# Two equal token groups and one pool of large tiles in a decoder step on one Trainium2 core

## The chip, the cores and the metric

The kernel runs on 1 core of one Trainium2 chip, in one launch. The metric is the device time of that launch in microseconds; the median of three runs stands for a kernel. The engines are called as the profile calls them: PE (TensorE), DVE (VectorE), ACT (ScalarE), POOL (GpSimd), SP (SyncE, which here only issues the weight loads).

## What is computed

One inference step of a decoder of two layers, all in fp32, for a prompt of 512 tokens and a sample of 8 sequences with 8 new tokens each (64). The model is 1024 wide. For each layer, cut from the reference:

```python
rq, rk, rv, rg, sq, sk, sv, mq, g_r, g_s, g_m = in_proj(x, w_in[l], pos)     # rotary on rq, rk, sq, sk
ret_o = retention(rq, rk, rv)              # 8 heads; the sample starts from a state that is given
swa_o = sliding_window(sq, sk, sv, sinks)  # 8 heads, 2 of keys and values, window 128
mem_o = mem_attend(mq, mk, mv)             # 4 heads, 256 memory tokens
ret_b = (silu(rg) * group_norm(ret_o)) @ w_br_ret
swa_b, mem_b = swa_o @ w_br_swa, mem_o @ w_br_mem
merged = sigmoid(g_r) * ret_b + sigmoid(g_s) * swa_b + sigmoid(g_m) * mem_b
x = layer_norm(ALPHA * x + merged @ w_out)
x = layer_norm(ALPHA * x + square(relu(x @ w_up)) @ w_down)
```

The prompt's memory keys and values come from `mem_prompt @ w_mem_kv`; each sample sequence has its own 256, cached, which are loaded. Outputs are the 576 tokens, and the new states, keys and values of each layer.

## The kernel before, in words

Features lie on partitions, tokens along the columns. All 576 tokens go through each weight once. The weights are cut into 154 units a layer (`unit_order`), 128 x 8 x 128 numbers each (512 KB). A unit is loaded by SP (`fetch`, 509) and split into a rounded high part and the rest, the low part (`split`, 515): a cast and a subtraction, or for `w_up` and `w_down` two casts and an accumulating DMA on POOL's queue. `gemm` (569) multiplies a unit by one group of tokens: for each of its 8 slices high by high, low by high and high by low, 24 matmuls that sum up in one PSUM bank. Three banks of tag g take turns for this.

The tokens stand in two groups (`NG`, `OFF`): A has the first 256 tokens of the prompt, B the other 256 and all 64 of the sample (320). `both` (589) runs a unit for A and then for B. The prompt's columns are worked on by `retention` (872), `swa_prompt` (1071) and `mem_prompt` (1202), the sample's by parts of `retention`, by `swa_sample` (1141) and `mem_sample` (1276), whose loads of cached keys (in_mck) and values (in_mcv) are issued on POOL's queue by `mem_load` (1260).

Large tiles come from two pools: tag A has 25 slots of 4096 bytes a partition (raw units, high parts, most low parts, everything of group A), tag B 15 of 5120 (everything of group B, and a few low parts by a rule in `split`). A new tile gets a slot that is free by the program's order, and what first writes it waits for the last reader of the tile before.

The order on each engine is made while the program is built. `run` (553) emits the matmul steps; after every sixth matmul of a unit it lets a filler advance, which gives out the next pieces of the branches, the norm and the weight splits, by a small clock of estimated times. Where an operation may run on two engines (`soonest`, 485; `pick`, 491; `rounded`, 495), that clock chooses: a subtraction goes to DVE or POOL, a cast to ACT or DVE. `plan` (204) estimates when each unit is used. So other widths change the order of many small operations and the engine of some. Between the layers the last norm of layer 0 (`norm_ev`) and the first units of layer 1 lie beside each other.

```python
def pick(self, *ins, bias=0.0):
    n = ins[0].free_size()
    return self.soonest((("vector", 0.068 + n / 960.0 + bias), ("gpsimd", 0.15 + n / 480.0)), *ins)
```

Of the kernel before, what the change touches and what calls it, by code (L numbers as in the profile page):

```python
# [17 lines left out]
P = 128  # L18
# [8 lines left out]
NG = {"A": 256, "B": 320}  # L27
OFF = {"A": 0, "B": 256}
# [14 lines left out]
N_A = 25  # L43
N_B = 15
# [89 lines left out]
def make_consts():  # L134
# [4 lines left out]
    pos = np.concatenate([np.arange(SEQ), np.tile(PAST + np.arange(NT), NB)]).astype(np.float32)  # L139
# [58 lines left out]

def mm_us(n):
    return n / 2400.0 + 0.0025  # L200


def plan():
    a, b = 24 * mm_us(256), 24 * mm_us(320)
    t, out = 0.0, []
    order = unit_order()
    for l in range(DEPTH):
        i = 0
        while i < UNITS:
            k = order[i][0]  # L210
            if k in ("mk", "mv"):
                out.append(t)
                t += a
# [4 lines left out]
            elif k == "rv":  # L218
                out += [t, t]
                t += 4.67 * a  # L220
# [195 lines left out]
class Builder:  # L416
# [35 lines left out]
    def u(self, n=320):  # L452
        return self.tile([P, 320], tag="u", bufs=5)[:, :n]

    def tt(self):
        return self.tile([P, 320], tag="t", bufs=4)
# [52 lines left out]
    def fetch(self, u):  # L509
        self.raw[u] = self.tile([P, 8, P], tag="A")  # L510
# [82 lines left out]
    def pair_tiles(self, dt=F32):  # L593
        return {"A": self.tile([P, 4, 256], dt, tag="A"), "B": self.tile([P, 4, 320], dt, tag="B")}

    def feat_tiles(self, nt):
        r = {}
        for g in "AB":
            r[g] = {"h": [], "l": []}
            for k in "hl":  # L600
                for j in range(nt):
                    r[g][k].append(self.tile([P, 4, NG[g]], F32R, tag=g))
        return r

    def load_x(self, X):
# [5 lines left out]
        def part(g, j):  # L611
            raw = self.tile([P, 4, NG[g]], tag=g)
# [9 lines left out]
        def split():  # L622
            for i in range(4):
# [5 lines left out]
                h = self.tile([P, 4, NG[g]], F32R, tag=g)  # L629
                lo = self.tile([P, 4, NG[g]], F32R, tag=g)  # L630
# [70 lines left out]
    def norm_ev(self, g, y, l, gi, eps, out, scale=None, bias=1.0):  # L701
# [33 lines left out]
        def half():  # L735
            c = st.pop("c")
            V.tensor_tensor(y[0], y[0], c.unsqueeze(1).to_broadcast([P, 4, n]), ALU.subtract)
            sq = self.tile([P, 4, n], tag=g)
# [7 lines left out]
        def last():  # L746
# [4 lines left out]
            t = self.tile([P, 320], tag="ln", bufs=2)[:, :n]  # L751
# [8 lines left out]
            r0 = self.tile([P, 320], tag="ln", bufs=2)[:, :n]  # L760
# [7 lines left out]
            a = self.tile([P, 320], tag="ln", bufs=2)[:, :n]  # L768
# [27 lines left out]
            if out is not None:  # L796
                out[g]["h"] += [self.tile([P, 4, n], F32R, tag=g) for _ in range(2)]
                out[g]["l"] += [self.tile([P, 4, n], F32R, tag=g) for _ in range(2)]
# [64 lines left out]

    def rope_evac(self, ps, out, o, n):
# [7 lines left out]
    def retention(self, l, p, qk, rv, sg, GR):  # L872
# [11 lines left out]
        yield Pe((qk, rv))  # L884
        v2 = self.tile([P, 2, 256], F32R)
        self.split_into(v2[:64, 0], v2[:64, 1], rv[:64, 4, :])
# [9 lines left out]
        for e in range(2):  # L896
            r = slice(e * 64, e * 64 + 64)
            for c in range(4):
                cs = slice(c * P, (c + 1) * P)
                T.matmul(pq[e][:, cs], lhsT=k[r, cs], rhs=q[r, cs], start=True, stop=True)  # L900
# [8 lines left out]
        for c in range(4):  # L909
            cs = slice(c * P, (c + 1) * P)  # L910
            T.transpose(pk[:, cs], k[:, cs], ident)
        px = [self.bank("a"), self.bank("a")]
        for e in range(2):
            r = slice(e * 64, e * 64 + 64)
            T.matmul(px[e][:64, P:P + 64], lhsT=k[r, 512:576], rhs=q[r, 512:576], start=True, stop=True)
        T.transpose(px[0][:64, 0:P], k[:, 512:576], ident)
# [17 lines left out]
        V.tensor_tensor(kq[:, 1].rearrange("p (c i) -> p c i", c=4), q[:, 0:512].rearrange("p (c i) -> p c i", c=4),  # L934
# [8 lines left out]
        for f in range(2):  # L943
            for e in range(2):
                r = slice(e * 64, e * 64 + 64)
                dst = self.qz[f * 64:f * 64 + 64, e, f * 32:f * 32 + 288].rearrange("p (b c) -> p b c", b=4)[:, :, 0:8]
                V.tensor_tensor(dst, q[r, 512 + f * 32:544 + f * 32].rearrange("p (b t) -> p b t", b=4),
# [11 lines left out]
        for bb in range(5):  # L959
            for e in range(2):  # L960
# [4 lines left out]
                else:  # L965
                    T.matmul(o, lhsT=ks[:, 256 + e * 64:320 + e * 64], rhs=rv[:64, 4, e * P:(e + 1) * P],
# [34 lines left out]
        gs = self.tile([P, P], tag="u", bufs=5)  # L1001
# [11 lines left out]
        wt = self.tile([P, 2, 512])  # L1013
        ws = self.tile([P, 2, 64], tag="ws", bufs=1)
# [763 lines left out]
```

## Time and profile before

| | |
|---|---|
| median of three runs | 2186.92 us (2186.02 to 2187.66) |
| profiled execution | 2185.91 us |
| its span | 2184.1 us |
| PE busy | 2147.9 us (98%) |
| DVE, ACT, POOL busy | 1060.2, 846.9, 411.2 us |
| HBM, read and written | 99 GB/s over the span |

The page has the span, each engine's busy time, the wait that ended an engine's idle time, and for each instruction its start and length. Matmuls are pipelined: the length of one overlaps the next, so their pace is read from start to start. The helper that records operations gives all of them one line, L331, so the rows are told apart by tile names and shapes (numbers left out). DVE and POOL rows of 128x1024 that read and write A are mostly the low parts of weight units.

### The profile page before, as it was taken

The page shows a single profiled execution, that of the slowest core. Times are in us where ns is not written, and L with a number is a line of the kernel's source. Part 1 is how long each engine was busy: PE and PEld are TensorE (multiplying, and loading weights), DVE is VectorE, ACT ScalarE, POOL GpSimd, SP SyncE. Part 2 cuts the span into 40 slices and gives each one's busy share as a digit, 9 for nine tenths or more (in the row PEclk, how much of TensorE's full clock was granted, in tenths as well). Part 3 has the DMA queues.
Part 4 walks back from the last instruction along what each step waited for, and adds up shares of the span by engine and source line. Part 5 has one row for each costly group of instructions (what it writes and reads, how often), then busy time and mean ns, then how long its engine had stood idle before and what let it go on. Part 6 is the DMA issues. An engine that isn't in the chain of part 4 may idle for free. (4 is left out here: it accounts for less than half of the span.)

```text
span 2184.1 us, 39229 instructions
## 1 busy us (share of the span) xinstructions
PE 2147.9 (98%) x16466; PEld 2089.6 (96%) x16466; DVE 1060.2 (49%) x2164; ACT 846.9 (39%) x1581; POOL 411.2 (19%) x400
## 2 busy tenths in 40 slices
PE   9999999999999999999999999999999999999996
PEld 9999999999999999999989998999999999999996
DVE  6666765455566111111876668554555751111127
ACT  3222234232146454636342221442221573636362
POOL 0222300011033111111432223000210321111113
PEclk9999999999999999999999999999999999999999
DMA  8222212334255867676452222123443557676661
GB/s 308 78 90 86 91 49 69 116 135 137 98 169 126 201 143 185 153 195 161 125 178 84 84 84 83 59 68 107 145 153 124 144 126 195 148 187 159 174 150 45
DMA packets 85168, 284.56 MB, mean 130 GB/s; under 512 B 9280, under 2 KB 19008, under 8 KB 84928
## 3 DMA queue, kind: packets, MB, share of 16 engines
q1 hardware_dynamic: 50944, 168.27, 22.2%
q0 software_dynamic: 28960, 105.92, 22.0%
q10 hardware_dynamic: 5088, 7.87, 1.1%
q8 instruction: 129, 2.11, 0.4%
q14 instruction: 47, 0.39, 0.1%
HBM read 200.89 MB, written 15.99 MB: 99 GB/s over the span
## 5 line engine op out<-in xcount | busy, mean ns | idle before, releaser
L331 PE MATMUL pg<-B,A 128*128 128x320 f32 x5920 | 1024.7, 310 | 2.4 <-DVE A L331 1.4
L331 PE MATMUL pg<-A,A 128*128 128x256 f32 (+1 forms) x6720 | 961.1, 286 | 12.1 <-DVE A L331 5.5
L331 PEld LDWEIGHTS pg<-A,A 128*128 128x128 f32 x6720 | 891.2, 192 | 28.9 <-issue 12.8
L331 PEld LDWEIGHTS pg<-B,A 128*128 128x128 f32 x5920 | 903.9, 188 | 7.5 <-issue 3.4
L331 ACT CAST A<-A 128x1024 fp32r<-128x1024 f32 (+4 forms) x316 | 294.0, 943 | 208.1 <-DVE A L331 73.1
L331 PE MATMUL pg<-A,B 128*128 128x256 f32 x1088 | 248.0, 283 | 0.0
L331 PE MATMUL pg<-B,B 128*128 128x320 f32 x704 | 217.5, 309 | 0.0
L331 DVE TENSOR_TENSOR A<-A,A 128x1024 fp32r<-128x1024 f32 (+3 forms) x173 | 191.1, 1115 | 49.6 <-ACT A L331 46.2
L331 PEld LDWEIGHTS pg<-A,B 128*128 128x128 f32 x1088 | 181.8, 192 | 0.0
L331 ACT ACTIVATE t<-pg 128x256 f32<-128x256 f32 (+1 forms) x128 | 52.5, 410 | 290.7 <-PE pg L331 290.5
L331 POOL TENSOR_TENSOR A<-A,A 128x1024 fp32r<-128x1024 f32 (+2 forms) x40 | 84.5, 2117 | 331.7 <-ACT A L331 273.6
L331 PEld LDWEIGHTS pg<-B,B 128*128 128x128 f32 x704 | 132.4, 188 | 0.0
L331 DVE TENSOR_TENSOR B<-u,B 128x320 fp32r<-128x320 f32 x80 | 39.4, 492 | 190.0 <-ACT B L331 190.0
L331 POOL DMA_DIRECT2D A<-A x64 | 55.7, 870 | 354.5 <-ACT u L331 177.1
L331 ACT ACTIVATE u<-pg 128x320 f32<-128x320 f32 (+1 forms) x128 | 51.4, 401 | 162.3 <-PE pg L331 162.1
L331 POOL DMA_DIRECT2D B<-A x64 | 55.0, 860 | 260.2 <-ACT B L331 115.8
L331 DVE TENSOR_TENSOR A<-u,A 128x256 fp32r<-128x256 f32 x72 | 30.5, 423 | 136.8 <-ACT A L331 129.0
L331 ACT ACTIVATE A<-A 128x1024 fp32r<-128x1024 f32 (+1 forms) x70 | 73.9, 1055 | 52.6 <-DMA B<-A 34.9
L331 DVE TENSOR_TENSOR B<-B,pg 128x320 f32<-128x320 f32 x56 | 27.0, 485 | 117.2 <-PE pg L331 117.1
L331 DVE TENSOR_TENSOR B<-B,u 128x256 f32<-128x256 f32 (+3 forms) x84 | 75.6, 908 | 2.4
L331 POOL TENSOR_TENSOR A<-A,cst 128x512 fp32r<-128x512 f32 x32 | 43.7, 1391 | 152.4 <-ACT A L331 152.4
L331 ACT ACTIVATE B<-A 128x1024 fp32r<-128x1024 f32 x64 | 67.4, 1053 | 0.0
(203 smaller groups left out, 1722.4 us busy)
## 6 DMA issues: line engine op xcount, KB each, us to landing
A<-in_wall SPq DMA_DIRECT2D x305, 512.0 KB, 3.5
B<-A POOLq DMA_DIRECT2D x64, 512.0 KB, 5.2
A<-A POOLq DMA_DIRECT2D x64, 512.0 KB, 5.3
A<-in_mck POOLq DMA_DIRECT2D x16, 512.0 KB, 4.2
A<-in_mcv POOLq DMA_DIRECT2D x16, 512.0 KB, 6.3
A<-in_s POOLq DMA_DIRECT2D x8, 512.0 KB, 4.1
out_state_s<-A POOLq DMA_DIRECT2D x8, 512.0 KB, 3.2
d<-A POOLq DMA_DIRECT2D x6, 512.0 KB, 7.7
```

The source lines that it names most:

```text
L331: r = f(*a, **kw)
```

## The change

The tokens are dealt anew: A holds the first 32 tokens of the sample and then 256 of the prompt, B the other 256 of the prompt and then the other 32 of the sample. Both groups are 288 wide. `POFF` says where the prompt begins in a group, `SOFF` where the sample does. The host puts inputs, rotary table and outputs in this order. All large tiles share one tag T with 38 slots of 4608 bytes. What reads the sample's columns now finds them at both ends: a copy gathers the keys in `retention` and for the output, the queries are copied in two parts, `stack` makes 16 copies of 32 columns instead of 8 of 64, the values of the sample get tiles of their own, and one half of `mem_sample` belongs to each group. The retention's result is split in two casts of 288 columns a head instead of three of 256, 256 and 64.

```diff
-NG = {"A": 256, "B": 320}
-OFF = {"A": 0, "B": 256}
+NG = {"A": 288, "B": 288}
+OFF = {"A": 0, "B": 288}
+POFF = {"A": 32, "B": 0}
+SOFF = {"A": 0, "B": 256}
...
-N_A = 25
-N_B = 15
+N_T = 38
...
+def by_group(prompt, sample):
+
+    return np.concatenate([sample[:32], prompt, sample[32:]], 0)
...
-    a, b = 24 * mm_us(256), 24 * mm_us(320)
+    a, b, c = 24 * mm_us(NG["A"]), 24 * mm_us(NG["B"]), 24 * mm_us(256)
...
-    def tile(self, shape, dt=F32, tag="A", bufs=None):
+    def tile(self, shape, dt=F32, tag="T", bufs=None):
         self.n += 1
-        bufs = bufs or {"A": N_A, "B": N_B}[tag]
+        if bufs is None:
+            tag, bufs = "T", N_T
...
     def fetch(self, u):
-        self.raw[u] = self.tile([P, 8, P], tag="A")
+        self.raw[u] = self.tile([P, 8, P])
...
     def split(self, u):
         raw = self.raw.pop(u)
         k = unit_order()[u % UNITS]
-        if k[0] == "wo":
-            b = True
-        elif k[0] in ("up", "dn"):
-            b = u % 2 == 0
-        else:
-            b = k[0] in ("gr", "br") and u % 4 == 0
-        tl = "B" if b else "A"
         hi = self.tile([P, 8, P], F32R)
-        lo = self.tile([P, 8, P], F32R, tag=tl)
+        lo = self.tile([P, 8, P], F32R)
...
+        qp, kp = q[:, 32:544], k[:, 32:544]
+        yield Pe((qk, rv, rvs))
+        qs, ksm = self.sample(q), self.u(64)
+        S.copy(ksm.rearrange("p (f t) -> p f t", f=2), self.sample(k))
...
-        for src, g_, a, b in ((wt[:, :, 0:256], "A", 0, 256), (wt[:, :, 256:512], "B", 0, 256), (ws, "B", 256, 320)):
-            hi, lo = GR[g_]["h"][h0 // 4][:, m:m + 2, a:b], GR[g_]["l"][h0 // 4][:, m:m + 2, a:b]
+        for g_ in "AB":
+            src = wt[:, :, OFF[g_]:OFF[g_] + NG[g_]]
+            hi, lo = GR[g_]["h"][h0 // 4][:, m:m + 2, :], GR[g_]["l"][h0 // 4][:, m:m + 2, :]
...
-        qz = self.tile([P, 4, 4, 32], tag="B")
+        g = "AB"[f]
+        cs = slice(SOFF[g], SOFF[g] + 32)
+        qz = self.tile([P, 4, 4, 32])
         for b in range(4):
-            V.tensor_tensor(qz[:, b], mq["B"][:, :, 256 + f * 32:288 + f * 32],
+            V.tensor_tensor(qz[:, b], mq[g][:, :, cs],
                             mm[:, b].unsqueeze(1).to_broadcast([P, 4, 32]), ALU.mult)
...
-                    S.copy(xs[:, 4 * j:4 * j + 4, 64 * i:64 * i + 64], X["B"][k][j][:, :, 256:320])
+                    for f, g in enumerate("AB"):
+                        S.copy(xs[:, 4 * j:4 * j + 4, 64 * i + 32 * f:64 * i + 32 * f + 32],
+                               X[g][k][j][:, :, SOFF[g]:SOFF[g] + 32])
```

Three places of the order show what moves. In the rows, the number behind a name is the tile's own.

PE at the first half of `mem_sample` in layer 0, before: the last of the six products of `mem_prompt`'s probabilities (A706, A707) with the values, the start of unit 62's group B, and after its 24 matmuls those with the four key tiles (A684, A685, A719, A720). A720 has the slot that A706 had.

```order
L331 MATMUL pa714_5157<-A706_5110,A633_4564 128x512
L331 MATMUL pa714_5157<-A706_5110,B634_4565 128x512
L331 MATMUL pa714_5157<-A707_5111,A633_4564 128x512
L331 MATMUL pg715_5165<-B63_361,A681_4949 128x320
...
L331 MATMUL pg715_5165<-B74_385,A681_4949 128x320
L331 MATMUL pa717_5186<-A684_4962,B716_5181 32x256 x4
L331 MATMUL pa717_5186<-A685_4964,B716_5181 32x256 x4
L331 MATMUL pa717_5186<-A719_5205,B716_5181 32x256 x4
L331 MATMUL pa717_5186<-A720_5211,B716_5181 32x256 x4
L331 MATMUL pg729_5236<-A443_3106,A700_5069 128x256
```

PE at the same place in the change: the end of unit 62's group B (T687 and T688 are the unit's high and low part), six matmuls of the next unit, and those with the four key tiles (T690, T691, T726, T727).

```order
L337 MATMUL pg721_5175<-T74_385,T688_4960 128x288
L337 MATMUL pg721_5175<-T75_386,T687_4959 128x288
L337 MATMUL pg725_5211<-T449_3115,T706_5068 128x288
L337 MATMUL pg725_5211<-T449_3115,T707_5069 128x288
L337 MATMUL pg725_5211<-T450_3116,T706_5068 128x288
L337 MATMUL pg725_5211<-T449_3115,T706_5068 128x288
L337 MATMUL pg725_5211<-T449_3115,T707_5069 128x288
L337 MATMUL pg725_5211<-T450_3116,T706_5068 128x288
L337 MATMUL pa723_5196<-T690_4972,T722_5191 32x256 x4
L337 MATMUL pa723_5196<-T691_4974,T722_5191 32x256 x4
L337 MATMUL pa723_5196<-T726_5222,T722_5191 32x256 x4
L337 MATMUL pa723_5196<-T727_5228,T722_5191 32x256 x4
```

The sample's products now stand six matmuls into the next unit. T727 has the slot that T688 had, and T688's last reader is the first row here.

DVE between the layers, before: the last two products of group B's norm, the low part of unit 162 (A_11829), the scaled parts of the norm (B_6560, B_6561) with their low parts, the low part of unit 164 (A_11887), and the next rotary step.

```order
L331 TENSOR_TENSOR B_6561<-B_6561,u_11762 128x640 x2
L331 TENSOR_TENSOR A_11829<-A_11802,A_11828 128x1024
L331 TENSOR_SCALAR B_6560<-B_6560,par_85 128x320 x2
L331 TENSOR_TENSOR B_11795<-B_6560,B_11793 128x640
L331 TENSOR_SCALAR B_6560<-B_6560,par_85 128x320 x2
L331 TENSOR_TENSOR B_11795<-B_6560,B_11793 128x640
L331 TENSOR_SCALAR B_6561<-B_6561,par_85 128x320 x2
L331 TENSOR_TENSOR B_11796<-B_6561,B_11794 128x640
L331 TENSOR_SCALAR B_6561<-B_6561,par_85 128x320 x2
L331 TENSOR_TENSOR B_11796<-B_6561,B_11794 128x640
L331 TENSOR_TENSOR A_11887<-A_11826,A_11886 128x1024
L331 STREAM_SHUFFLE u_11950<-pg_11909 128x256
```

DVE at the same place in the change, where T_11861 is the low part of unit 162, T_11934 that of 163 and T_11952 that of 164.

```order
L337 TENSOR_TENSOR T_6571<-T_6571,u_11787 128x576 x2
L337 TENSOR_TENSOR T_11861<-T_11824,T_11860 128x1024
L337 TENSOR_SCALAR T_6570<-T_6570,par_85 128x288 x2
L337 TENSOR_TENSOR T_11811<-T_6570,T_11809 128x576
L337 TENSOR_SCALAR T_6570<-T_6570,par_85 128x288 x2
L337 TENSOR_TENSOR T_11811<-T_6570,T_11809 128x576
L337 TENSOR_SCALAR T_6571<-T_6571,par_85 128x288 x2
L337 TENSOR_TENSOR T_11812<-T_6571,T_11810 128x576
L337 TENSOR_SCALAR T_6571<-T_6571,par_85 128x288 x2
L337 TENSOR_TENSOR T_11812<-T_6571,T_11810 128x576
L337 TENSOR_TENSOR T_11934<-T_11836,T_11933 128x1024
L337 TENSOR_TENSOR T_11952<-T_11858,T_11951 128x1024
```

The low part of unit 163 has come over from POOL, and stands behind the norm's twelve products. Further up and not shown, a step towards the mean of group B (t, 288 columns) has come to DVE as well, behind the low parts of units 157 and 158; POOL did it before.

POOL at the local queries of layer 0, before: outputs, the low part of unit 36 (A_2816), outputs, the retention's low parts (A_1370, B_1372), and the low parts of units 38, 39 and 40. Layer 1 has the same with units 190 to 194.

```order
L331 DMA out_swv_p<-B_2507 128x128
L331 DMA out_swv_s<-B_2507 64x128
L331 TENSOR_TENSOR A_2816<-A_2544,A_2815 128x1024
L331 DMA out_swk_p<-u_2870 128x128
L331 DMA out_swk_s<-u_2870 64x128
L331 TENSOR_TENSOR A_1370<-A_2843,A_1369 128x512
L331 TENSOR_TENSOR B_1372<-ws_2844,B_1371 128x2x64
L331 TENSOR_TENSOR A_2967<-A_2813,A_2966 128x1024
L331 TENSOR_TENSOR A_3033<-A_2928,A_3032 128x1024
L331 TENSOR_TENSOR B_3099<-A_2964,A_3098 128x1024
```

POOL at the same place in the change: T_2906 is the low part of unit 37.

```order
L337 DMA out_swv_p<-T_2512 128x128
L337 DMA out_swv_s<-svs_2513 64x128
L337 DMA out_swk_p<-u_2870 128x128
L337 DMA out_swk_s<-u_2870 64x128
L337 TENSOR_TENSOR T_2906<-T_2704,T_2905 128x1024
L337 TENSOR_TENSOR T_1375<-T_2875,T_1374 128x576
L337 TENSOR_TENSOR T_2976<-T_2830,T_2975 128x1024
L337 TENSOR_TENSOR T_3042<-T_2903,T_3041 128x1024
L337 TENSOR_TENSOR T_3108<-T_2973,T_3107 128x1024
```

Unit 36's subtraction has gone to DVE, unit 37's has come from DVE to the head of the row of subtractions, and the retention's piece is one of 576 columns (2 x 288).

## Rows read from the trace of the kernel before

**Rows 1.** the page's part 1, each engine: busy us, share, instructions

```profile
PE 2147.9 (98%) x16466; PEld 2089.6 (96%) x16466; DVE 1060.2 (49%) x2164; ACT 846.9 (39%) x1581; POOL 411.2 (19%) x400
```

**Rows 2.** windows of 50 us: stretch, length, busy by engine, clock, DMA

```profile
800.00:850.00 50.00, 50.00 (x377) 50.00 (x376) 7.30 (x16) 29.74 (x46) 9.10 (x11) 1.00 0.81 192
1100.00:1150.00 50.00, 45.58 (x323) 43.97 (x323) 35.96 (x46) 19.36 (x31) 17.09 (x14) 0.97 0.45 158
```

**Rows 3.** TensorE's waits: who, for whom, us in total, times, longest

```profile
PE pg L331 <- DVE A L331: 6.9, 4, 4.4
PE pg L331 <- DVE u L331: 1.9, 2, 1.0
PE pa L331 <- DMA A<-in_mck: 1.3, 2, 1.0
```

**Rows 4.** groups by form, TensorE: count, busy us, mean ns, idle before

```profile
L331 PE MATMUL pg<-B,A 128*128 128x320 f32 x5920 | 1024.7, 310 | 2.4 <-DVE A L331 1.4 <-DVE B L331 1.0
L331 PE MATMUL pg<-B,B 128*128 128x320 f32 x704 | 217.5, 309 | 0.0
```

**Rows 5.** timeline, TensorE in the MLP: start us, us, instruction, count

```profile
805.45 3.04 PE L331 MATMUL pg<-A,A 128*128 128x256 f32 x24
808.33 3.69 PE L331 MATMUL pg<-B,A 128*128 128x320 f32 x24
811.85 0.28 PE L331 MATMUL pg<-A,A 128*128 128x256 f32 x1
```

**Rows 6.** timelines, TensorE and POOL at `mem_sample`, layer 0; page's DMA list

```profile
469.85 0.40 PE L331 MATMUL pa<-A,A 128*128 128x512 f32 x1
471.23 3.68 PE L331 MATMUL pg<-B,A 128*128 128x320 f32 x24
474.84 1.50 PE L331 MATMUL pa<-A,B 128*32 128x256 f32 x24
477.30 0.64 PE L331 MATMUL pa<-A,B 128*32 128x256 f32 x8 [0.96 <-DMA A<-in_mck]
...
471.47 0.53 POOL L331 DMA_DIRECT2D A<-in_mck  x1 [0.79 <-PE pa L331]
...
A<-in_mck POOLq DMA_DIRECT2D x16, 512.0 KB, 4.2
```

**Rows 7.** timelines, TensorE, VectorE and POOL between the layers

```profile
1112.23 1.44 PE L331 MATMUL pg<-A,A 128*128 128x256 f32 x5 [4.42 <-DVE A L331]
1115.02 5.35 PE L331 MATMUL pg<-A,A 128*128 128x256 f32 x42
...
1108.80 3.37 DVE L331 TENSOR_TENSOR A<-A,A 128x1024 fp32r<-128x1024 f32 x1
...
1118.38 1.22 DVE L331 TENSOR_TENSOR A<-A,A 128x1024 fp32r<-128x1024 f32 x1
...
1108.50 2.59 POOL L331 TENSOR_TENSOR A<-A,A 128x1024 fp32r<-128x1024 f32 x1 [4.03 <-ACT A L331]
```

**Rows 8.** timelines, VectorE and POOL at the local gates, layer 0

```profile
505.65 3.09 DVE L331 TENSOR_SCALAR A<-A,md 128x256 f32<-128x256 f32 x4
...
505.30 2.50 POOL L331 TENSOR_TENSOR A<-A,A 128x1024 fp32r<-128x1024 f32 x1 [7.08 <-ACT A L331]
```

**Rows 9.** timelines, VectorE, POOL and TensorE at the local queries, layer 1

```profile
1345.04 6.77 DVE L331 TENSOR_TENSOR B<-B,u 128x320 f32<-128x320 f32 x1
...
1358.47 0.49 DVE L331 TENSOR_TENSOR B<-B,u 128x320 f32<-128x320 f32 x1
...
1349.06 2.39 POOL L331 TENSOR_TENSOR A<-A,A 128x1024 fp32r<-128x1024 f32 x1
...
1353.13 3.79 PE L331 MATMUL pg<-B,A 128*128 128x320 f32 x24 [1.38 <-DVE A L331]
```

**Rows 10.** timelines, TensorE's last matmul and VectorE behind it

```profile
2170.23 0.61 PE L331 MATMUL pa<-s,ones 128*128 128x256 f32 x2
...
2171.29 3.35 DVE L331 TENSOR_TENSOR A<-A,u 128x1024 f32<-128x1024 f32 x1
```

More of the change, by code (lines that the diff above doesn't have):

```diff
@@ L593, in pair_tiles @@
     def pair_tiles(self, dt=F32):
-        return {"A": self.tile([P, 4, 256], dt, tag="A"), "B": self.tile([P, 4, 320], dt, tag="B")}
+        return {g: self.tile([P, 4, NG[g]], dt) for g in "AB"}
     def feat_tiles(self, nt):
@@ L601, in feat_tiles @@
                 for j in range(nt):
-                    r[g][k].append(self.tile([P, 4, NG[g]], F32R, tag=g))
+                    r[g][k].append(self.tile([P, 4, NG[g]], F32R))
         return r
@@ L750, in last @@
             yield (p1,)
-            t = self.tile([P, 320], tag="ln", bufs=2)[:, :n]
+            t = self.tile([P, 288], tag="ln", bufs=2)[:, :n]
             S.activation(t, p1, AF.Square)
@@ L767, in last @@
             yield (r0,)
-            a = self.tile([P, 320], tag="ln", bufs=2)[:, :n]
+            a = self.tile([P, 288], tag="ln", bufs=2)[:, :n]
             V.tensor_tensor(a, r0, r0, ALU.mult)
@@ L796, in last @@
             if out is not None:
-                out[g]["h"] += [self.tile([P, 4, n], F32R, tag=g) for _ in range(2)]
-                out[g]["l"] += [self.tile([P, 4, n], F32R, tag=g) for _ in range(2)]
+                out[g]["h"] += [self.tile([P, 4, n], F32R) for _ in range(2)]
+                out[g]["l"] += [self.tile([P, 4, n], F32R) for _ in range(2)]
             z = [mult(i) for i in range(4)]
@@ L862, in norm_ev, with sample @@
         return ev
+    @staticmethod
+    def sample(x):
+        return x.rearrange("p (k t) -> p k t", t=32)[:, 0:18:17]
     def rope_evac(self, ps, out, o, n):
@@ L899, in retention @@
                 cs = slice(c * P, (c + 1) * P)
-                T.matmul(pq[e][:, cs], lhsT=k[r, cs], rhs=q[r, cs], start=True, stop=True)
+                T.matmul(pq[e][:, cs], lhsT=kp[r, cs], rhs=qp[r, cs], start=True, stop=True)
         yield (pq[0], rc)
@@ L910, in retention @@
             cs = slice(c * P, (c + 1) * P)
-            T.transpose(pk[:, cs], k[:, cs], ident)
+            T.transpose(pk[:, cs], kp[:, cs], ident)
+        yield Pe((ksm,))
         px = [self.bank("a"), self.bank("a")]
@@ L914, in retention @@
             r = slice(e * 64, e * 64 + 64)
-            T.matmul(px[e][:64, P:P + 64], lhsT=k[r, 512:576], rhs=q[r, 512:576], start=True, stop=True)
-        T.transpose(px[0][:64, 0:P], k[:, 512:576], ident)
+            T.matmul(px[e][:64, P:P + 64], lhsT=ksm[r], rhs=qs[r], start=True, stop=True)
+        T.transpose(px[0][:64, 0:P], ksm, ident)
         yield (pk,)
@@ L1000, in retention @@
         gn = self.tile([P, 2, 4, P])
-        gs = self.tile([P, P], tag="u", bufs=5)
+        gs = self.u(P)
         nb = self.small(9, "rnb")
@@ L1012, in retention @@
         yield Pe((gn, gs))
[L1013 to L1014 removed]
+        wt = self.tile([P, 2, TOK])
         gg = self.par[:, l, 32 + h0:34 + h0]
@@ L1188, in swa_sample @@
                 d = slice(kv * 64, kv * 64 + 64)
-                T.matmul(po[d, 0:P], lhsT=sv[fr, 4, d], rhs=pn[fr, kv, :], start=True, stop=False,
+                T.matmul(po[d, 0:P], lhsT=svs[fr, d], rhs=pn[fr, kv, :], start=True, stop=False,
                          tile_position=(f * 32, kv * 64))
@@ L1289, in mem_sample @@
         den = self.small(1, "zd")
-        p = self.tile([P, 256], tag="u", bufs=5)
+        p = self.u(256)
         yield (ps,)
@@ L1317, in mem_sample @@
                 vt.append(self.mem_load("mcv", l, f * 4 + b + 2))
-        o = self.tile([P, P], tag="u", bufs=5)
+        o = self.u(P)
         yield (po,)
@@ L1503, in gen @@
                 def gen():
-                    yield Pe((sk[:, 384:576],))
+                    ss = self.u(64)
+                    yield (sk,)
+                    S.copy(ss.rearrange("p (f t) -> p f t", f=2), self.sample(sk))
+                    yield Pe((ss,))
                     pt = self.bank("a")
-                    T.transpose(pt[:, 0:P], sk[:, 384:512], ident)
-                    T.transpose(pt[:64, P:2 * P], sk[:, 512:576], ident)
+                    T.transpose(pt[:, 0:P], sk[:, 416:544], ident)
+                    T.transpose(pt[:64, P:2 * P], ss, ident)
                     t = self.u(256)
@@ L1552, in mem_parts @@
                 nc.scalar.dma_start(t, src)
-                parts += [self.tile(src.shape, F32R, tag=k) for k in ("AB" if src is mvd else "BB")]
+                parts += [self.tile(src.shape, F32R) for _ in range(2)]
                 yield (t,)
@@ L1604, in load_y @@
             for g in "AB":
-                y[g] = [self.tile([P, 4, NG[g]], tag=g) for _ in range(2)]
+                y[g] = [self.tile([P, 4, NG[g]]) for _ in range(2)]
                 for j in range(2):
```

118 lines of the change are left out of this document (60 added, 58 removed).

## The prediction

> **What bounds the kernel.** I read the page first: TensorE is busy for 2147.9 of 2184.1 us, the other engines for half of it or less [rows 1]. That leaves 36.2 us without a matmul in the whole span, and no change of group sizes can win more than that unless a matmul itself gets cheaper or dearer. Two stretches of 50 us show where the rest lies: in the MLP (800 to 850) TensorE is busy for all 50.00 us, between the layers (1100 to 1150) for 45.58 [rows 2]. So in most of the program only the pace of the matmuls counts, and at a few places a wait does. The list of waits names them: the longest are for VectorE's results (6.9 us on tiles A in 4 waits, 1.9 on u in 2), and 1.3 us for the loads of the cached memory keys, in_mck [rows 3]. A clock of 1.00 in the stretch of the MLP says that TensorE ran at 2.4 GHz there [rows 2].
>
> **The matmuls.** The change gives every weight unit two groups of 288 columns instead of 256 and 320. The 6624 matmuls of group B stand in two rows, 5920 and 704 [rows 4], and group A has as many. Their pace, from start to start: 24 of 256 columns take 808.33 − 805.45 = 2.88 us (120.0 ns each), 24 of 320 take 811.85 − 808.33 = 3.52 us (146.7 ns) [rows 5]. That is 26.7 ns for 64 columns, so 288 lies at 133.3 ns on that line, and the pair costs 266.7 ns before and after. Term: 0. What could make it another number is in the rivals.
>
> **The sample's memory keys (+3.6).** `mem_sample` multiplies four key tiles by the queries, 8 matmuls for each tile. Before, the fourth tile's load was issued at 471.47, when the probabilities of `mem_prompt` (A_5110), whose slot it takes, had been read by the 512-column matmuls from 469.85 on; TensorE then worked through 24 matmuls of group B, ran the first 24 sample matmuls in 1.50 us and waited 0.96 us before the last 8 at 477.30, which is 5.83 us after the issue [rows 6]. In the one pool the fourth tile gets the slot of T688, the low part of unit 62. The order of the change shows that this is read until the last matmul of unit 62's group B, 6 matmuls of group A (0.80 us at 133.3 ns) ahead of the sample's. So the tile is wanted 0.80 + 1.50 = 2.3 us after its slot is free. If it takes 5.83 us again, TensorE waits 3.5 us, 2.6 more than now; if it takes the 4.2 us of the page's median landing [rows 6], 1.9 us, 0.9 more. I take the middle, 1.8, and twice, since the second layer repeats the order: +3.6, between +1.8 and +5.2. The values' loads stand behind this one on POOL's queue and come later too; they are used later still, and I put them at nothing, up to +1 for each layer.
>
> **Between the layers (−1.1).** The longest wait, 4.42 us before 1112.23, is for the low part of unit 162 (VectorE, 1108.80, 3.37 us) [rows 7]. The same subtraction alone takes 1.22 us (1118.38); at 1108.80 POOL's subtraction for unit 163 ran beside it (1108.50, 2.59 us) [rows 7]. The change puts unit 163's on VectorE, behind group B's norm (second pair of order fences), so the first should take 1.22: −2.15. The norm products ahead of it are a tenth narrower: by the 0.49 us of 320 columns [rows 9], and nearly two and three times that for 640 and 1280, the six last make some 5 us, so −0.5. But unit 163's low part now comes late. Twelve products lie between; before, from the end of unit 162's (1108.80 + 3.37 = 1112.17) to 1118.38 they took 6.2 us [rows 7], so a tenth less, 5.6, and its own 1.2 make 6.8 us after unit 162's. TensorE wants it when 8 mean matmuls and the rest of unit 162's group are done: before, 1115.02 − 1112.23 = 2.8 us and 18 matmuls of 120 ns, 5.0 in all, now about 5.4. That is a new wait of 1.4 to 1.5 us. Sum −1.1. Ends: −4.4, if nothing takes the wait's place, and +2.4, if a step for B's mean, which POOL did and which now stands on VectorE behind two subtractions (1.22 each), pushes the whole chain back.
>
> **The local branch's gates (−1.5).** The two waits for u, 1.9 us together [rows 3], stand in the two layers where a product on VectorE was stretched to 3.09 us for four of 256 columns beside POOL's subtraction of 2.50 [rows 8]. The change does that subtraction on VectorE. The waits should go, but VectorE gets 1.2 us of work there, in time that the stretch took before. I take −1.5, between −1.9 and 0.
>
> **The local queries (0).** This stage has TensorE wait for VectorE's rotary products. One of them took 6.77 us from 1345.04, where its like took 0.49 at 1358.47; POOL ran without a break until 1351.45 (1349.06 + 2.39) [rows 9]. So a VectorE operation on two SBUF tiles can be held until POOL's run ends. The Trainium skill (GPSIMD Engine Reference, section 1, Specifications) says that POOL's SBUF interfaces are shared with VectorE, with contention when VectorE has two SBUF inputs; this row agrees, and by that rule whoever lengthens POOL's run lengthens VectorE's wait. The change takes one subtraction away ahead of POOL's run and puts one into it, and does more rotary products before the run starts (third pair of order fences). Fewer products are left to be held, each perhaps for longer: 0, with −1.4 a layer at the one end (a wait like the one of 1.38 us before 1353.13 goes [rows 9]), +4.8 at the other (second rival).
>
> **The tail (+1.2) and small copies (+0.2).** After the last matmul only group A's norm is left, and A grows by an eighth. From 2170.84, the end of the last matmul (2170.23 + 0.61), to 2184.1 it is 13.3 us, mostly elementwise work like the product of 1024 columns at 2171.29, 3.35 us [rows 10]. An eighth of 13.3 is 1.7, the upper end; issue and the output's landing do not grow, so +1.2. The narrower copies (the sample's keys, eight more copies when the sample is stacked, one more transpose a layer) go to ScalarE, which is idle for most of the span [rows 1]; only TensorE's transposes count, +0.2. If ScalarE were late, its casts would be; those lie ahead of their use in most units.
>
> **Sum.** 0 + 3.6 − 1.1 − 1.5 + 0 + 1.2 + 0.2 = +2.4 us. The profiled execution took 2185.91 us, so 2188.3; it lay 1.0 below the median of the three runs shown (2186.92), and against that the number is 2189.3, say 2189. A measurement of this kernel can tell about 0.2% (4.4 us) from no change, so this is no change.
>
> **The rivals.**
> 1. *The waits go and nothing takes their place* (faster). The gaps between the layers (4.4), for u (1.9) and one at the local queries of each layer (2 × 1.4) vanish, the memory keys cost only their lower end (+1.8), and tail and copies stay (+1.4): −5.9, so 2181. For it: five large subtractions fewer run on POOL, beside which VectorE is slow [rows 7 to 9]. Against: unit 163's new place. Chance 0.22.
> 2. *POOL's run holds VectorE* (slower). At the local queries two subtractions more can fall into POOL's run, the low part of unit 191 at its head and unit 194's at its end, each 2.4 us like the one at 1349.06 [rows 9]: 6.4 us (1345.04 to 1351.45) become up to 11.2. If VectorE's first operation on two SBUF tiles waits for all of it, as it did at 1345.04, it is held up to 4.8 us longer, nothing empties TensorE's three banks meanwhile, and TensorE loses up to 4.8 us in each layer. It decides from the point where the hold outlasts what three groups of matmuls take (3 × 3.2 = 9.6 us). With +2.4 from the rest and two thirds of the two holds (6.4): +8.8, 2196. Against it: more products are done before the run. Chance 0.27.
> 3. *288 is charged as 320.* The widths of the groups in the trace (256, 320, 512) are all multiples of 64. If the array's time went up in such steps, a pair would cost 293.3 ns, 26.7 more, 6624 times: +177 us, 2364. Nothing in the rows speaks for steps; chance 0.02.
> 4. *The 120 ns are a floor.* If a 256-column matmul were held up by its weight load, 288 would cost less than the line says. The 512-column matmuls bound it: six from 469.85 to 471.23 are 230 ns each [rows 6]. From 146.7 at 320, that is 0.434 ns a column, so 132.8 ns at 288, and a pair of 265.6: 1.1 ns less, 6624 times, −7 us, and 2182 with the sum's +2.4. The Trainium skill (TensorE: Matmul & The Clock Gate, Back-to-back issue gap) says that in a stream the spacing is set by the weight load and the matmul both; the rows show no sign of it at 256. Chance 0.03.
>
> **How the numbers follow.** My forecast has 0.46. Its own range, from the ends of the larger terms taken half way, is 2184 to 2194. To leave no more than 2 in 10 out, the range must reach rivals 1 and 2: 2181 to 2197. Faster by over 0.2% (below 2182.5): rival 1 and 4 almost whole, and a little of the forecast's low end, 0.25. Slower by over 0.2% (above 2191.3): rival 2 for the most part, rival 3 and the forecast's upper end, 0.33. The rest, 0.42, is the same.
>
> **What would show it.** In the profile of the change: 24 matmuls of 288 columns in 3.20 us from start to start, in both groups. A wait of TensorE for in_mck of 2 to 3.5 us in each layer. Between the layers the wait for unit 162 down to about 2 us and another right behind it, at unit 163. No wait for u at the local branch's gates. At the local queries waits of 1 to 2 us as now, and a VectorE operation that lasts as long as POOL's run. From the last matmul to the end 14.5 us. I am wrong if the pace is not 133.3 ns, if in_mck stays at 1 us (the slot was free in time), or if TensorE loses over 5 us at the local queries.

## The result: 0.86% slower, and where the time went

| | before | change |
|---|---|---|
| median of four runs | 2187.29 us (2186.02 to 2188.34) | 2206.38 us (2201.67 to 2209.66) |
| ratio | | 1.0086, 95% interval 1.0067 to 1.0105 |
| profiled execution, span | 2185.91, 2184.1 us | 2201.67, 2199.6 us |
| mean granted clock of it | 0.997 | 0.994 |

The time lies above the range of the prediction. The other three runs of the change had a mean clock of 0.992, 0.992 and 0.990 (2206.75, 2206.0 and 2209.66 us); the profiled one is the quickest, and the profiled one of before was quick too, so the two traces lie 15.5 us apart where the medians lie 19.

The pace of the matmuls is what was forecast: 160 of them, of both groups, start within 21.2 us (21.49 less the last one's 0.3), 133 ns apart. TensorE's timeline in the MLP, to be held against [rows 5]:

```profile
803.77 21.49 PE L337 MATMUL pg<-T,T 128*128 128x288 f32 x160
```

So the 15.5 us between the two spans are waits and clock. This table has the end of the last matmul of a unit in both traces, in us; a step is what the stage added to the change's distance from before:

| up to unit | stage before it | before | change | step |
|---|---|---|---|---|
| 35 | start, retention | 265.2 | 264.5 | −0.7 |
| 38 | local queries | 288.3 | 291.2 | +3.6 |
| 57 | gates, sliding window | 435.5 | 438.5 | +0.1 |
| 81 | memory stage | 615.9 | 624.4 | +5.5 |
| 145 | output projection, MLP | 1029.6 | 1036.9 | −1.2 |
| 164 | between the layers | 1139.9 | 1150.2 | +3.0 |
| 189 | retention | 1348.9 | 1358.9 | −0.3 |
| 192 | local queries | 1373.0 | 1385.9 | +2.9 |
| 235 | gates, memory stage | 1700.0 | 1718.0 | +5.1 |
| 299 | output projection, MLP | 2113.8 | 2130.1 | −1.7 |
| end of the last matmul | last units | 2170.8 | 2185.2 | −1.9 |
| end of the span | last norm | 2184.1 | 2199.6 | +1.1 |

The same three stages lose in both layers or between them: local queries 6.5, memory stages 10.6, between the layers 3.0. The list of TensorE's waits of the change names what it waited for there (who, for whom, us in total, times, longest); in [rows 3] the keys stood with 1.3 us and the values not at all:

```profile
PE pg L337 <- DVE T L337: 15.9, 10, 4.2
PE pa L337 <- DMA T<-in_mck: 4.2, 4, 1.8
PE pa L337 <- DMA T<-in_mcv: 3.2, 2, 1.8
PE pg L337 <- ACT T L337: 2.1, 2, 1.3
PE pa L337 <- DVE T L337: 2.0, 6, 0.4
PE pa L337 <- DVE accA L337: 1.3, 1, 1.3
```

At the local queries the timelines of POOL, VectorE and TensorE show in layer 0:

```profile
259.47 10.81 POOL L337 TENSOR_TENSOR T<-T,T 128x1024 fp32r<-128x1024 f32 x5
...
260.61 10.00 DVE L337 TENSOR_TENSOR u<-u,rope 128x288 f32<-128x288 f32 x1
...
271.90 11.92 PE L337 MATMUL pg<-T,T 128*128 128x288 f32 x78 [4.17 <-DVE T L337]
```

POOL's outputs held its queue until 259.47; five subtractions had gathered behind them and ran without a break for 10.81 us. A product of 0.45 us on VectorE began at 260.61 and ended 0.33 us after that run. It lasted longer than three groups of matmuls (9.6 us); TensorE stood for 4.17 us, where it had waited 1.84 before. Layer 1 repeats it (9.98 and 4.15 us). This is the second rival.

Layer 0 of before needs a second look. POOL ran there without a break as well, for 9.73 us (261.36 to 271.09), and yet VectorE got four operations with two SBUF inputs through beside it, at 2 to 3 us each. The kernel before with a skew of 6 (below) has the same instructions up to this place, and in its trace the first of these operations was held for the whole run:

```profile
263.04 5.49 POOL L331 TENSOR_TENSOR A<-A,A 128x1024 fp32r<-128x1024 f32 x2
...
263.37 2.90 DVE L331 TENSOR_TENSOR B<-A,B 128x512 fp32r<-128x512 f32 x1
...
268.85 2.52 DVE L331 TENSOR_TENSOR A<-A,u 128x256 f32<-128x256 f32 x1
```

```profile
261.34 9.11 DVE L331 TENSOR_TENSOR B<-B,u 128x320 f32<-128x320 f32 x1
```

TensorE then waited 3.71 us, and the stage lost 3.4 us against the trace of before. So in layer 0 the run on POOL was nearly as long before, and the +3.6 is to a large part the difference between an execution in which VectorE takes turns with POOL and one in which it is held. In layer 1 the run itself grew, from 6.45 to 10.81 us. Which of the two comes how often is not shown; the two traces with the change's full run (the change, and the one with a key slot of its own) have the hold in both layers.

At the memory stage, POOL and TensorE in layer 0 (answering to [rows 6]):

```profile
478.27 0.55 POOL L337 DMA_DIRECT2D T<-in_mck  x1 [1.67 <-issue]
494.30 1.10 POOL L337 DMA_DIRECT2D T<-in_mcv  x2 [0.30 <-POOL T L337]
...
482.45 0.64 PE L337 MATMUL pa<-T,T 128*32 128x256 f32 x8 [1.80 <-DMA T<-in_mck]
498.82 0.64 PE L337 MATMUL pa<-T,T 128*32 128x128 f32 x16 [1.43 <-DMA T<-in_mcv]
```

The fourth key tile comes 4.2 us after its issue and TensorE waits 1.80 us, as worked out; that the last two value tiles cost 1.43 us more was put at nothing to 1. They stand on POOL's queue behind a subtraction (491.63) that waits for ScalarE's cast of its unit.

Between the layers the longest wait of the change is not at unit 162 but ahead of it, for one of two low parts that VectorE makes behind the last scaled parts of group A's norm (TENSOR_SCALAR with par). VectorE had itself stood for POOL just before:

```profile
1097.45 0.46 DVE L337 TENSOR_TENSOR rc<-rc,u 128x288 f32<-128x288 f32 x1 [1.59 <-POOL rc L337]
...
1099.32 0.77 DVE L337 TENSOR_SCALAR T<-T,par 128x288 f32<-128x288 f32 x2
...
1102.44 0.86 PE L337 MATMUL pg<-T,T 128*128 128x256 f32 x5 [2.68 <-DVE T L337]
```

These last scaled parts begin 62 us after the end of unit 145; before it was 54 (1083.40).

The clock is seen in windows of 10 us (stretch, length, busy by engine, clock, DMA share, GB/s); before, only 1110 to 1120 had less than 1.00 ahead of the last matmuls:

```profile
260.00:270.00 10.00, 7.73 (x59) 7.50 (x57) 10.00 (x3) 4.08 (x5) 10.00 (x5) 1.00 0.27 95
270.00:280.00 10.00, 8.10 (x51) 8.10 (x52) 8.21 (x25) 0.00 (x0) 0.29 (x1) 0.83 0.16 52
480.00:490.00 10.00, 8.19 (x57) 7.33 (x58) 5.34 (x17) 1.61 (x3) 0.07 (x1) 0.83 0.69 256
1120.00:1130.00 10.00, 7.92 (x47) 7.53 (x47) 9.86 (x19) 8.34 (x19) 4.40 (x7) 0.83 0.81 304
1360.00:1370.00 10.00, 5.85 (x34) 5.61 (x34) 9.90 (x16) 0.00 (x0) 4.67 (x3) 0.85 0.14 49
```

A clock of 0.83 to 0.85 over 10 us means that TensorE ran a part of them at 1.2 GHz, and that 1.5 to 1.7 us of full speed are missing in each of the stretches; the first of them, from 260, still has 1.00. The runs differ by it: the mean clock of 0.994 to 0.990 is 13.2 to 22.1 us of full speed missing from spans of 2199.6 and 2207.7 us, 8.9 between them, and their times lie 8.0 apart. (The clock is given to a thousandth, so each of these can be 1 us off; and in the profiled run about half of the 13.2 lies behind the last matmul, where it costs TensorE nothing.) In before it is 6.6 (0.003 of 2184.1).

### The profile page after: what moved, and what is told of

The parts are those of the page before. It is cut to its first block, busy times and chain, and to the rows that moved or that the text cites. A ratio compares the mean times of both kernels' runs of the same rounds, so it can differ in the third digit from the quotient of the medians.

```text
span 2199.6 us, 39261 instructions
## 1 busy us (share of the span) xinstructions
PE 2153.1 (98%) x16468; PEld 2091.5 (95%) x16468; DVE 1071.2 (49%) x2186; ACT 847.7 (39%) x1581; POOL 388.2 (18%) x384
## 4 chain that ended last, share of the span: by engine, by line
PE 87%; DVE 8%; DMA 2%; issue 1%; ACT 1%; POOL 1%; SPq 0%; DVEq 0%; POOLq 0%; ACTq 0%
PE pg L337 78%; PE pa L337 9%; DVE T L337 4%; DVE u L337 2%; ACT T L337 1%; DMA T<-in_mcv 0%; DVE ln L337 0%; DMA T<-in_wall 0%; DMA T<-in_mck 0%; POOL T L337 0%; DMA T<-T 0%; DMA T<-in_swk 0%; DMA T<-in_memT 0%; ACT u L337 0%; DVE accA L337 0%
## 5 line engine op out<-in xcount | busy, mean ns | idle before, releaser
L337 PE MATMUL pg<-T,T 128*128 128x288 f32 (+1 forms) x14432 | 1958.3, 296 | 18.2 <-DVE T L337 15.9
L337 PEld LDWEIGHTS pg<-T,T 128*128 128x128 f32 x14432 | 1925.0, 188 | 41.4 <-DVE T L337 18.2
L337 ACT CAST T<-T 128x1024 fp32r<-128x1024 f32 (+5 forms) x358 | 307.7, 883 | 267.3 <-issue 83.7
L337 DVE TENSOR_TENSOR T<-T,T 128x1024 fp32r<-128x1024 f32 (+5 forms) x248 | 271.7, 1104 | 83.1 <-ACT T L337 71.9
L337 POOL DMA_DIRECT2D T<-T x128 | 110.6, 864 | 616.6 <-ACT T L337 517.1
L337 POOL TENSOR_TENSOR T<-T,T 128x1024 fp32r<-128x1024 f32 (+2 forms) x43 | 91.3, 2135 | 413.0 <-ACT T L337 350.8
L337 ACT ACTIVATE T<-T 128x1024 fp32r<-128x1024 f32 (+1 forms) x140 | 148.7, 1064 | 24.4 <-DMA T<-T 11.8
L337 PE MATMUL pa<-T,T 128*32 128x128 f32 (+8 forms) x1064 | 121.7, 319 | 9.5 <-DMA T<-in_mck 4.2
L337 PEld LDWEIGHTS pa<-T,T 128*32 128x32 f32 (+3 forms) x1064 | 83.5, 148 | 32.4 <-issue 15.0
L337 DVE TENSOR_TENSOR T<-T,u 128x288 f32<-128x288 f32 (+2 forms) x132 | 92.8, 713 | 4.0 <-POOL accB L337 0.3
```

Of the source, the lines that this page charges most:

```text
L337: r = f(*a, **kw)
```

## The experiments

The kernel before was timed beside every group of experiments, and its median moved between 2187.6 and 2189.7 us. So kernels are compared by their ratio to it. No run has one half of the change alone, the equal groups or the one pool.

**The local queries.** Theory: POOL's run holds VectorE and the clock falls behind the wait. Rivals: VectorE's own load, or the widths. Three subtractions are taken out of the run:

```diff
-            self.split_into(hi, lo, raw, True)
+            self.split_into(hi, lo, raw, True, u % UNITS in (37, 38, 39))
...
-        e = self.pick(hi) if flexible else self.nc.vector
+        e = self.pick(hi) if flexible and not dve else self.nc.vector
```

> The changed kernel, but the low parts of the second to fourth unit after the third rotary query unit (37, 38, 39 and 191, 192, 193) are made on VectorE, so POOL's unbroken run at the local queries is 2 pieces of 576 columns and 1 subtraction, some 5 us, in place of 10.8. Theory (POOL's run holds VectorE, TensorE's banks fill, the clock falls behind the stall): VectorE's held product lasts about 4.5 us, TensorE's waits of 4.2 us and the half clock at 270 and 1360 go, about 3.6 us less in each layer and 7 in all: 2199. Rival (the wait there is VectorE's own load): VectorE gets 3 subtractions of 1.2 us more in each layer, TensorE waits as long or longer: 2206 or more.

Measured: 2194.39 us, ratio 1.0021 (1.0011 to 1.0031), 0.65% or 14 us less than the change, twice what was expected; in the traces the two stages take 5.7 and 6.0 us less. POOL and VectorE in layer 0:

```profile
261.71 3.22 POOL L337 TENSOR_TENSOR T<-T,T 128x576 fp32r<-128x576 f32 x2 [1.28 <-ACT T L337]
265.12 3.16 POOL L337 TENSOR_TENSOR T<-T,T 128x1024 fp32r<-128x1024 f32 x1 [0.19 <-ACT T L337]
...
263.57 2.45 DVE L337 TENSOR_TENSOR T<-T,T 128x1024 fp32r<-128x1024 f32 x1
```

Nothing on VectorE lasts over 2.5 us there, TensorE has no wait at all in either layer, and VectorE's added 3.7 us cost nothing. So the subtractions on POOL were the cause. The same in the kernel before, with units 38 and 39 alone:

> The kernel before, with the low parts of units 38, 39, 192 and 193 on VectorE instead of POOL: POOL's run at the local queries falls from 6.4 to about 4 us. Theory (POOL's run holds VectorE): VectorE's products there last under 4.5 us, TensorE's waits of 1.3 to 2.2 us shrink, 1 to 2 us less in each layer: 2184. Rival (VectorE's own load): no change or 1 us more a layer, 2187 to 2189.

Measured: 2182.51 us, ratio 0.9966 (0.9953 to 0.9979), better than expected, by 7 us where the two stages of the trace gain 5.1 (the trace of before has the turns in layer 0, other executions may not). TensorE's waits for VectorE on tiles B fall from 5.2 us to:

```profile
PE pg L331 <- DVE B L331: 2.2, 3, 1.1
```

If runs on POOL are bad, none at all might be best; `pick` then returns VectorE always:

> The changed kernel with every subtraction that the planner may place (pick) on VectorE; POOL keeps its DMAs and a few fixed pieces. Theory (POOL's runs hold VectorE): no product on VectorE over 4 us at the local queries, TensorE's longest wait for VectorE under 2 us there, between the layers too; with VectorE's 35 more subtractions of 1.2 us it is busy for about 1100 us; about 10 us less, 2196. Rival (VectorE becomes the bound where units come fast): new waits of TensorE for low parts of units, 2210 or more.

Measured: 2231.11 us, ratio 1.0191 (1.0176 to 1.0206): the rival. At the local queries TensorE has no wait, but now weights and loads come late at other places, and the clock falls to 0.985. Its waits:

```profile
PE pg L337 <- DVE T L337: 17.5, 10, 5.5
PE pg L337 <- DMA T<-T: 13.6, 4, 5.1
PE pa L337 <- DMA T<-in_mcv: 8.5, 4, 3.9
PE pa L337 <- DMA T<-in_mck: 8.4, 4, 4.0
```

**The memory stage.** Theory: the pool has no slot free in time. Before there were 25 + 15 = 40 slots, now there are 38. First, a slot of its own for the fourth key tile (the second edit moves the sample's local values into the tiles rvs):

```diff
-        t = self.tile([P, 4, 256] if name == "mck" else [P, 2, 512])
+        own = dict(tag="key", bufs=1) if name == "mck" and b % 4 == 3 else {}
+        t = self.tile([P, 4, 256] if name == "mck" else [P, 2, 512], **own)
...
-        svs = self.tile([64, P], tag="svs", bufs=1)
+        svs = self.tile([64, 256], tag="rvs", bufs=2)[:, 0:P]
```

> The changed kernel, but the fourth tile of the cached memory keys has a slot of its own. Theory (the slot comes free too late): its load is issued right behind the third's, 1.7 us earlier, TensorE's last wait for in_mck falls from 1.8 to about 0.3 us, and with it the half clock behind it: 1.5 to 3 us less in each of the layers, 2201. Rival (the loads are late because POOL's queue stands still behind the third tile, or the transfer itself is slower): less than 0.5 us a layer, 2206.

Measured: 2204.29 us, ratio 1.0066 (1.0051 to 1.0082), 0.2% less than the change, between the two, and not clear of noise (the interval of the change begins at 1.0067). The issue follows the third's at once, and part of the wait goes on to the values:

```profile
PE pa L337 <- DMA T<-in_mcv: 4.1, 2, 2.4
PE pa L337 <- DMA key<-in_mck: 1.5, 2, 0.8
PE pa L337 <- DMA T<-in_mck: 0.8, 2, 0.4
```

Together with the three low parts:

> The changed kernel with both edits, the three low parts on VectorE at the local queries and a slot of its own for the fourth key tile. Theory (two separate losses, each with half clock behind it): they add, 0.65% and 0.2% off the change's ratio of 1.0086, so 1.000 of before, 2188 where before is 2189. Rival (the keys' gain is only moved to the wait for the values behind it, which saw 4.1 us in the kernel with the own slot alone): no better than the three low parts alone, 1.002.

Measured: 2189.66 us, ratio 1.0008 (0.9998 to 1.0017). They add nearly as expected, though the intervals of this and of the three low parts alone overlap. To see whether slots are the cause, less is kept in the pool, once by splitting two units ahead (`run(self, steps, cap=2)`), once by fetching one raw unit ahead (`self.split_next + 1` in `feed`), both with the three low parts on VectorE:

> The changed kernel with the three low parts on VectorE, and units split at most two ahead of the one in use, not three: a high and a low part less in the pool. Theory (at the sample's memory stage loads wait for slots): the waits of TensorE for in_mck and in_mcv, 9.0 us with the three low parts, fall under 5, some 3 to 6 us less, ratio 0.999 to 1.001. Rival (POOL's queue order and the transfer's length make them): the same 9 us, and late weights on top, 1.003 or more.

> The changed kernel with the three low parts on VectorE, and raw units fetched one ahead of the one split, not two: one raw tile less in the pool, splits as before. Theory (slots): the 9.0 us of waits for in_mck and in_mcv fall to about 6, ratio about 1.001. Rival (slots are not it): 9 us as before, and if a fetch comes late TensorE waits for in_wall, 1.003 or more.

Measured: 2210.73 us, 1.0107 (1.0093 to 1.0120), and 2205.49, 1.0082 (1.0068 to 1.0096). The total is that of the rivals, and the waits are more than the theory asked: of the 9.0 us for keys and values 0.2 and 0.3 are left. What takes their place are splits that come late (cap 2, first fence) and the accumulating DMAs of the MLP's weights (one ahead, second fence):

```profile
PE pg L337 <- DVE T L337: 17.1, 20, 2.7
PE pg L337 <- ACT T L337: 13.4, 10, 1.4
...
PE pa L337 <- DMA T<-in_mck: 0.2, 1, 0.2
```

```profile
PE pg L337 <- DMA T<-T: 12.4, 4, 3.6
...
PE pa L337 <- DMA T<-in_mcv: 0.3, 1, 0.3
```

So slots were the cause, and one raw unit less is needed in that stage alone:

```diff
-        while self.dma_next <= min(self.split_next + 2, len(self.use) - 1):
+        ahead = 1 if 58 <= self.split_next % UNITS < 78 else 2
+        while self.dma_next <= min(self.split_next + ahead, len(self.use) - 1):
```

> The changed kernel with the three low parts on VectorE, and raw units fetched one ahead of the one split in the memory stage alone (units 58 to 77 of each layer), two ahead elsewhere. Theory (in the memory stage the one pool is short of slots for the loads): the 9.0 us of waits for in_mck and in_mcv fall under 1 as with one ahead everywhere, the accumulating DMAs of the MLP are on time as before (no wait for T<-T over 0.5 us), 8 to 12 us less than the three low parts alone: ratio 0.997 to 0.999. Rival (one ahead brings late weights in that stage too): 1.001 or more.

Measured: 2183.21 us, ratio 0.9974 (0.9964 to 0.9984). The wait for values is 0.7 us, for keys none of note and for T<-T none. For the keys it is the issue that comes earlier, not the transfer that gets shorter: in layer 0 the fourth tile is issued 0.55 us behind the third (1.98 with the three low parts alone), at a median of 4.3 us to landing (3.9). For the values both change: the third tile is issued 0.85 us behind the start of the values' products instead of 2.2, and the median falls from 6.9 to 5.8. Whether two more slots would do the same was not tried. With these two edits the change is quicker than the kernel before. Its list of waits begins:

```profile
PE pg L337 <- DVE T L337: 9.2, 9, 2.7
```

**Between the layers.** Of that 9.2 us 8.5 lie there: from unit 145 to 164 this kernel takes 6.0 us more than before, 3.0 more than the change itself (the wait at unit 163 is 2.70 us instead of 1.11, and the clock falls twice instead of once). Theory: cover. Group A's last norm runs beside 7 groups of B, 24.6 us before and 22.4 now, and is itself an eighth longer. `DN_SKEW = 8` gives it 8 groups; it was run on two bases, and the opposite (6) on the kernel before:

> As the kernel with one ahead in the memory stage, and the last units of layer 0's down projection skewed by 8 instead of 7. Theory (of the 3 us lost between the layers most is cover: group A's norm, an eighth longer, runs beside 7 groups of B of 3.2 us, 22.4, where it had 7 of 3.52, 24.6): with 25.6 us the norm is done in time, TensorE's waits between 1075 and 1130 fall by 2 to 3 us: ratio 0.0012 lower. Rival (the wait there comes from the split of weights behind B's norm, or from POOL): no change from the kernel without it.

> As the kernel with the three low parts and the own key slot (ratio 1.0008), with the skew of 8. Theory (cover): 2 to 3 us less, 0.9996. Rival: 1.0008, or more, since a skew of 8 keeps one more unit's weights in the pool.

> The kernel before with a skew of 6 instead of 7 in layer 0: group A's norm has 6 groups of B of 3.52 us, 21.1, for cover instead of 24.6. Theory (cover): it loses 2 to 4 us between the layers, ratio 1.001 to 1.002. Rival (the norm of A is not what the weights wait for there): within 1 us, 1.000.

Measured: 2187.85 us, 0.9995 (0.9986 to 1.0005); 2194.29, 1.0024 (1.0014 to 1.0033); and 2193.7, 1.0021 (1.0011 to 1.0030). The third is what the theory asks: unit 145 to 164 takes 3.2 us longer. (Its trace also lost 3.4 us to the hold at the local queries, in which the skew has no part.) In the first two the expectation fails, and TensorE's timeline with skew 8 shows a wait that is new:

```profile
1052.74 0.45 PE L337 MATMUL pg<-T,T 128*128 128x288 f32 x1 [3.51 <-ACT T L337]
1058.55 9.37 PE L337 MATMUL pg<-T,T 128*128 128x288 f32 x53 [5.36 <-DMA T<-T]
```

Unit 153's cast starts only at 1051.7, since `run` lets 7 units be split ahead and the skew now asks for 8. With that mended (`7 if X2 else 8` becomes `8`, on the base with one ahead in the memory stage):

> As the kernel with skew 8, with units split up to eight ahead there instead of seven, so that unit 153 is split before it is needed. Theory (cover for group A's norm): the wait of 5.4 us for T<-T with the 3.5 us ahead of it and the half clock at 1050 go, and what the longer cover saved stays: the stretch from unit 145 to 164, which took 6.0 us more than before with skew 7 and one ahead in the memory stage, takes 3 us more at most, ratio 0.996. Rival (the loss between the layers is not cover): the stretch takes 6 us more again, ratio 0.9974 as with skew 7.

Measured: 2175.94 us, ratio 0.9939 (0.9922 to 0.9956). From unit 145 to 164 it takes 2.7 us less than before, 8.7 less than with skew 7, no stretch there has half clock, and its list of waits begins

```profile
PE pg L337 <- DVE T L337: 5.5, 7, 1.7
```

The last scaled parts of A's norm begin 56 us after unit 145, where it was 62 with skew 7, 59 in before with skew 6, and 54 in before. So the loss between the layers was cover; a limit of eight with a skew of 7 was not run, so what the limit alone does is open. This version is 0.6% quicker than the kernel before and 1.5% quicker than the change.

Last, the wait that the prediction looked at, in the kernel before (on top of units 38 and 39): unit 162's low part on POOL.

> The kernel before with units 38, 39, 192 and 193 on VectorE and the low part of unit 162, between the layers, on POOL. Theory (unit 162's subtraction is late because it stands behind group B's norm on VectorE, and with the wait goes the half clock behind it): POOL makes it from about 1104.5 to 1107, when TensorE wants it; the wait of 4.4 us falls under 1.5, and 3 to 5 us go: ratio 0.9945, 2177. Rival (POOL's longer run holds the norm on VectorE, 2.4 us, and what needs the norm is late): ratio 0.997, as with the two low parts alone.

Measured: 2181.48 us, ratio 0.9971 (0.9959 to 0.9982), no different from 0.9966: the rival. The wait of 4.4 us goes, but ahead of unit 163 TensorE waits 2.73 us for a PSUM bank. ScalarE's copy out of it stands behind the norm's scaled parts and the cast of unit 163, and the norm is late since POOL's run of three subtractions (7.95 us) holds two of its products on VectorE for 5.84 us; the half clock stays, too:

```profile
1110.69 1.05 ACT L331 COPY A<-pg 128x512 f32<-128x512 f32 x2
...
1111.31 5.49 PE L331 MATMUL pg<-A,A 128*128 128x256 f32 x24 [2.73 <-ACT A L331]
```

## Why the prediction was wrong, step by step

Three terms failed: the local queries, put at 0, cost 6.5 us; the values, put at nothing, made TensorE wait for 3.2 us; and the stage between the layers, put at −1.1, cost 3.0. The half clock behind the waits was in no term.

- **The matmuls, 0.** Right: 133 ns. The rivals on steps of 64 columns and on a floor are out.
- **The sample's memory keys, +3.6.** Right for the keys: their wait grew from 1.3 to 4.2 us, by 2.9, inside the bounds. The step that failed is the sentence that put the values at nothing: 3.2 us. With small waits for VectorE (2.0 and 0.9), half clock at 480 (1.7), and less the gates' wait (1.9), this makes 9 of the 10.6 us that the two stages lost, where keys and gates together had +2.1; the rest is not named. That slots were the cause is shown by one raw unit less (9.0 to 0.3 us).
- **Between the layers, −1.1.** Wrong in sign, +3.0. What I looked at came out (unit 162's low part takes 1.22 us): TensorE waits 1.32 and 0.97 us at unit 162, and 1.11 at 163 (1.4 to 1.5 forecast):

```profile
1119.74 0.40 PE L337 MATMUL pg<-T,T 128*128 128x288 f32 x1 [1.32 <-ACT T L337]
1121.11 1.44 PE L337 MATMUL pg<-T,T 128*128 128x288 f32 x5 [0.97 <-DVE T L337]
...
1128.15 6.13 PE L337 MATMUL pg<-T,T 128*128 128x288 f32 x44 [1.11 <-DVE T L337]
```

  But "narrower by a tenth" was applied to B's norm alone. A's norm got wider, and the groups of B that cover it got shorter, by 2.2 us in all; its end came late, and with it the low parts behind it, for which TensorE waits 2.68 us at 1102.44. The skews of 6 and 8 show that this decides.
- **The local branch's gates, −1.5.** Right as to the wait: none for u is left in TensorE's matmuls of weights. Its size was not measured apart from the memory stage.
- **The local queries, 0.** The step that failed first. The second rival had the mechanism, the place and the point (a hold beyond 9.6 us) and a price of up to 4.8 us a layer; the hold was 10.0 us and the loss 3.6 and 2.9. Its chance was 0.27, and its time, 2196, still lay 10 us too low. I set the products moved ahead of the run against it. That did not help: the first operation on two SBUF tiles behind them was held, and all behind it with it. The order had shown five subtractions in a row, and [rows 9] that a row of them can hold VectorE. It had shown five in a row in layer 0 of before as well, and [rows 9] are of layer 1: that layer 0 got off with 1.84 us was the luck of an execution with turns, and the prediction did not ask whether it would come again.
- **The tail, +1.2.** Right: from 2185.17 (2184.52 + 0.65) to 2199.6 it is 14.4 us (14.5 forecast).

```profile
2184.52 0.65 PE L337 MATMUL pa<-s,ones 128*128 128x288 f32 x2
...
2185.65 3.73 DVE L337 TENSOR_TENSOR T<-T,u 128x1152 f32<-128x1152 f32 x1
```

- **Not in the sum at all: the clock.** Every term took a wait at its length. The second stretch of [rows 2] had shown 0.97, where the one long wait is. The quickest run of the change has three such places more, of 1.5 to 1.7 us each. The slowest run has 8.9 us less of full speed than the quickest.

The stages that gained (output projection −1.2 and −1.7, the last units −1.9) were in no term. In the last layer A's groups cover B's norm, and there A got longer and B's norm narrower, so the same rule would say a gain; this was not tried.

## What to carry to other kernels

When group widths change and the sum of the matmuls stays, look at what each group covers: the work that hides behind a group of matmuls is timed by that group's length. Merging pools changes which tile's last reader a load waits for; count the slots in the stage that holds the most tiles, and prefetch less there rather than everywhere. On an engine that is nearly always busy, add to each wait of several us the slow matmuls behind it. A stage that gets through beside a long run of POOL in one trace need not do so in the next execution.

## What the runs showed of the hardware that was not expected

- A VectorE operation with two SBUF inputs can be held not for one POOL subtraction but for all that follow without a break: 10.00 us beside a run of 10.81, 6.77 beside 6.45 [rows 9], 9.11 beside 8.77. The same instructions can also take turns: beside a run of 9.73 us four such operations took 1.95 to 2.90 us each, and POOL's subtractions 2.6 to 2.8 instead of 2.4. What decides between the two is not shown. With the three low parts on VectorE, POOL's work there comes in pieces with breaks of 0.2 to 1.3 us, and the longest VectorE operation is 2.45 us.
- TensorE's clock falls to 1.2 GHz behind waits of 4.17 and 4.15 us, and in the same trace also where two shorter waits stood close together (0.36 and 1.80 us at 480 to 490, 1.32 and 0.97 us at 1120). It does not always follow a shorter wait: the change waits 2.68 us at 1102.44 and has 1.00 behind it, the kernel with one ahead in the memory stage waits 2.69 us at the same place and has half clock. Each kernel has one trace, so where the other runs of the change lost theirs is not seen; their mean clocks (0.994 to 0.990) go with times 8 us apart. Where no wait is longer than 1.7 us (skew 8 with the limit of eight), four runs lie between 2175.66 and 2176.32 us.
